# Head products in two steps of 256 tokens, eight gating products on VectorE, two gate projections in score banks

## The chip, the cores and the metric

The kernel runs on one core of one Trainium2 chip. The metric is the device time of one execution in microseconds (us). TensorE is called PE, VectorE DVE, ScalarE ACT, GpSimd POOL, SyncE SP.

## The reference

Two layers over 1024 tokens of width 1024, each wrapped as `x <- x + rmsnorm(mixer(rmsnorm(x)))`. Layer 0 is sliding-window attention (16 query heads of 64, 2 key heads, window 128, a sink per head, rotation of a quarter of each head), layer 1 a gated recurrence of 8 heads. The change lies in layer 0:

```
def attention_mixer(h, positions, w_in, b_in, sinks, w_out, b_out):
    proj = h @ w_in + b_in
    q, k, v, z = jnp.split(proj, [ATTN_WIDTH, ATTN_WIDTH + KV_WIDTH, ATTN_WIDTH + 2 * KV_WIDTH], axis=-1)
    q = partial_rope(q.reshape(B, T, N_HEADS, HEAD_DIM), positions)
    k = partial_rope(k.reshape(B, T, N_KV_HEADS, HEAD_DIM), positions)
    v = v.reshape(B, T, N_KV_HEADS, HEAD_DIM)
    o = sliding_window_gqa(q, k, v, sinks)
    return (o * jax.nn.silu(z)) @ w_out + b_out
```

## The kernel before

Every float32 operand of a matmul is split into a high and a low part in a rounded format, `hi` and `lo`, and every product is three matmuls: hi by hi, hi by lo, lo by hi (`product`, L185 to L189).

**Weights.** They are 132 slices of 128 x 512 (256 KB). `fetch` (L131 to L135) loads them over SP's queue into four raw buffers `wraw`. `advance` (L137) splits a slice: POOL makes `whi` for the first 20 slices (L152), ACT afterwards; DVE makes `wlo` (L155), POOL for slices 2 and 3. The parts go to ten places `whi`, `wlo`; `used` frees a place after its last product and advances.

**Activations.** The 1024 tokens are two halves of 512. A half is loaded as four tiles of 128 rows (`x_load`, L254; the fourth in two pieces), squared on ACT (L976), turned into `rstd` on POOL (`rstd_of`, L215 and L217) and scaled on DVE (`norm_rows`). `transpose_half` (L232 to L240) then transposes it on PE, four blocks to a PSUM bank `pst`, for eight blocks k of the model width; `act_from_psum` evicts each as `acth` (ACT, L179) and `actl` (DVE, L180).

**Products.** `proj_feat` holds weights fixed and moves 512 tokens: 24 matmuls of 128 x 512 into one of two PSUM banks tagged `mm`. The units are `v_unit` (values), `q_unit` (queries; their parts `qh`, `ql` go to DRAM, `qd`), `k_unit`, `z_unit` (gate). There are also two banks each with tags `t`, `s` and `o`; those with `s` hold the attention's scores.

**Head.** At the end of `emit` (L960 to L985) stand the loads of constants, positions and the first half of x, a flag by which the program branches, the squares and `rstd` of all four tiles, and the loads of the first four slices. Behind the branch come the norms, all 32 transposes, then `v_unit(0)` and `q_unit(0, 1, 0)`, which use slices 0, 1 and 2, 3. The loads of the other half of x, `xh`, are issued right behind the branch.

**Attention and gate.** `attn(g, b)` works on one of two groups of heads and one of eight blocks of 128 queries: scores (L528, L529), softmax, transposes, masks as four to six selects on POOL (L560 to L568), products with the values (L571 to L575), and the output `ob` (L576, L577). Other units are put between the blocks by a list (`fill`, `at`). `z_unit(p, half)` makes the gate's 128 columns p for one half: ACT's tanh (L483), `th` scaled on POOL (L484), DVE's product with z (L488), and the product with the output, `o * th`, on POOL (L490). The units p = 4 to 7 for half 0 are the last ones; where p >= 4 and half 1, the gate comes first and `attn` multiplies by the output afterwards, again on POOL (L579).

The instruction order of each engine comes from a scheduler, which places instructions by priority and readiness; `tc.high_priority` lifts some. A wrapper `v` keeps DVE's instructions in the order of the program. Each engine takes its instructions in order.

Of the kernel before, what the change touches and what calls it, by code (L numbers as in the profile page):

```python
# [12 lines left out]
F32 = mybir.dt.float32  # L13
# [5 lines left out]
ALU = mybir.AluOpType  # L19
# [70 lines left out]
def emit(tc, I, out):  # L90
    nc = tc.nc
    v = InOrder(tc, nc.vector)
    from contextlib import ExitStack
    top = ExitStack()
    with top:
# [32 lines left out]
        W_K = 10  # L128
        W = {"split": 0, "fetch": 0, "left": {}, "place": {}, "dmas": {}, "split_ins": {}, "actl": {}, "free": list(zip(whi, wlo))}

        def fetch(end):  # L131
            while W["fetch"] < min(end, NS):
                f = W["fetch"]
                W["dmas"][f] = nc.sync.dma_start(wraw[f % NR], I["w"][f])
                W["fetch"] += 1  # L135

        def advance(end=NS):  # L137

            while W["split"] < end:
                i = W["split"]  # L140
                fetch(i + NR)
                if i in (W_K, W_K + 1):
                    W["place"][i] = W["keys"][i - W_K]
                elif W["free"]:
                    W["place"][i] = W["free"].pop(0)
                else:
                    return
                raw, (hi, lo) = wraw[i % NR], W["place"][i]
                with hp():
                    on_pool = i in (2, 3)  # L150
                    if i < 20:
                        nc.gpsimd.tensor_scalar(hi, raw, 1.0, 1.0, op0=ALU.mult, op1=ALU.mult)  # L152
                    else:
                        nc.scalar.activation(hi, raw, AF.Copy)  # L154
                    W["split_ins"][i] = (nc.gpsimd if on_pool else v).tensor_tensor(lo, raw, hi.bitcast(F32), op=ALU.subtract)  # L155
                W["split"] += 1
# [19 lines left out]

        def act_from_psum(k, half, ps, scale):
            hi, lo = act[k, half]
            ins = nc.scalar.activation(hi, ps, AF.Copy, scale=scale)  # L179
            W["actl"][k] = v.scalar_tensor_tensor(lo, ps, scale, hi.bitcast(F32), op0=ALU.mult, op1=ALU.subtract)  # L180
            return ins
# [8 lines left out]

        def proj_feat(first, half):

            ps = mm()
# [17 lines left out]
        def rstd_of(pool, ms, width, eps=EPS, pinned=False):  # L211

            m = pool.tile([P, width], F32, tag="ms", bufs=4, name="ms")
            keep = tc.keep_in_program_order if pinned else lambda ins: ins
            keep(nc.gpsimd.tensor_scalar(m, ms, eps, 1.0, op0=ALU.add, op1=ALU.mult))  # L215
            r = pool.tile([P, width], F32, tag="rstd", bufs=4, name="rstd")
            W["rstd"] = keep(nc.gpsimd.tensor_tensor(r, m, nhalf[:, :width], op=ALU.pow))  # L217
            return r
# [34 lines left out]

        def x_load(xh, half):  # L254
            for j in range(4):
# [85 lines left out]
        def layer0():  # L341
# [15 lines left out]

            def q_unit(g, ct, half):
                ps = proj_feat(12 + 2 * ct if g else 2 * ct if ct else 8, half)
                with hp():  # L360
# [24 lines left out]
            with pool("start", "right") as sp:  # L385
# [5 lines left out]
                at = iter([1, 2, 3, 4])  # L391
                some = lambda: [steps.pop(0)() for _ in range(next(at))]
                with tc.high_priority(offset=1000):
                    v.on = True
                    hn0 = []
                    for j in range(4):
                        some()
                        for cs in halves(j):
                            norm_rows(sp, o0[:, j, cs], o0[:, j, cs], rs0[j])
                        hn0.append(o0[:, j, :])  # L400
# [36 lines left out]

                def v_unit(half):
                    ps = proj_feat(0, half)
                    vf = qp.tile([P, 512], F32, tag="th", bufs=2, name="vf")  # L440
# [26 lines left out]

                v_unit(0)
                q_unit(0, 1, 0)
                transpose_half(hn1, 1, C_PRE)  # L470
# [7 lines left out]
            with pool("att", "right") as ap:  # L478
                def z_unit(p, half):
                    ps = proj_feat(20 + 2 * (p ^ 4), half)  # L480
                    with hp():
                        th = qp.tile([P, 512], F32, tag="th", bufs=2, name="th")
                        nc.scalar.activation(th, ps, AF.Tanh, bias=hbias[:, 10 + p:11 + p], scale=0.5)  # L483
                        nc.gpsimd.tensor_scalar(th, th, 0.5, 0.5, op0=ALU.mult, op1=ALU.add)  # L484
                        o = og[p // 4][:, p % 4, half * 512:(half + 1) * 512]

                        early = p >= 4 and half == 1
                        v.scalar_tensor_tensor(o if early else th, ps, bias(10 + p), th, op0=ALU.add, op1=ALU.mult)  # L488
                        if not early:
                            nc.gpsimd.tensor_tensor(o, o, th, op=ALU.mult)  # L490

# [15 lines left out]
                def attn(g, b):  # L507
# [70 lines left out]
                    if g and b >= 4:  # L578
                        nc.gpsimd.tensor_tensor(ogb, ogb, ob, op=ALU.mult)  # L579

# [389 lines left out]
        v.tensor_copy(flag, ld[:1, :1])  # L970
        rs0 = []
        for j in range(4):
            ms = const.tile([P, 2], F32, tag="ss2", bufs=4, name="ss2")
            cut = halves(j)
            for i, cs in enumerate(cut):
                nc.scalar.activation(wraw[2 + j % 2].bitcast(BF16)[:, cs], o0[:, j, cs], AF.Square, scale=D ** -0.5,  # L976
                                     accum_out=ms[:, i:i + 1])
            if len(cut) > 1:
                nc.gpsimd.tensor_scalar(ms[:, :1], ms[:, :1], EPS, 1.0, op0=ALU.add, op1=ALU.mult)
            rs0.append(rstd_of(const, ms[:, len(cut) - 1:len(cut)], 1, ms[:, :1] if len(cut) > 1 else EPS))  # L980
        fetch(NR)
        go = nc.values_load(flag[0:1, 0:1])
# [79 lines left out]
```

## Time and profile before

| what | us |
| --- | --- |
| median of 3 runs | 911.94 (910.14 to 912.55) |
| profiled execution | 911.3 |
| its span in the trace | 909.5 |
| PE busy | 885.2 (97%) |
| DVE, ACT, POOL busy | 553.8, 378.1, 341.3 |

The profile is one execution. Times in it count from the span's start. A row of a timeline has the start, the duration, the engine and line, what is written from what, the shape, and in brackets the idle time before it with what ended it. A row of a group has the count, the busy time and mean nanoseconds of one, and the idle before. A row of the waits has the total, the count and the longest.

### The profile page before, as it was taken

To read this page: it belongs to the slowest core of one execution; us is meant where nothing else is said; L and a number is where in the kernel's file an instruction comes from. 1 tells how busy PE (TensorE), PEld (TensorE's weight loads), DVE (VectorE), ACT (ScalarE), POOL (GpSimd) and SP (SyncE) were. 2 spreads that over 40 slices of the span, in tenths; PEclk is the share of its full clock that TensorE was granted. 3 is DMA by queue.
4 is the path that set the end of the run, shared out by engine and by line. 5 is a ranking of instruction groups with operands and counts; after the bars stand their busy time and mean duration, and the time that the engine had idled before them with its cause. 6 is when DMAs were issued, how large, how long until landed. Compare 5 with 4: busy or idle time off the path is not lost.

```text
span 909.5 us, 14370 instructions
## 1 busy us (share of the span) xinstructions
PE 885.2 (97%) x5342; PEld 737.4 (81%) x5342; DVE 553.8 (61%) x911; ACT 378.1 (42%) x982; POOL 341.3 (38%) x506
## 2 busy tenths in 40 slices
PE   5999999999999999999999999999999999999996
PEld 4888888888887788878888888888888788888885
DVE  6879888777776435762268774246867924252343
ACT  6526667666666332542323341433334224251311
POOL 5514456658787103330054432115425433220011
PEclk9999999999999999999999999999999999999998
DMA  8546364522212223540311010121111002032053
GB/s 286 156 145 185 104 185 129 150 56 82 82 45 58 92 74 129 171 150 12 109 54 37 25 47 1 51 67 35 36 48 48 1 1 93 1 105 82 24 184 120
DMA packets 53608, 78.63 MB, mean 86 GB/s; under 512 B 4824, under 2 KB 25048, under 8 KB 53528
## 3 DMA queue, kind: packets, MB, share of 16 engines
q1 hardware_dynamic: 53248, 77.48, 27.7%
q8 instruction: 44, 0.72, 0.3%
q14 instruction: 36, 0.29, 0.1%
q10 hardware_dynamic: 280, 0.13, 0.1%
HBM read 58.89 MB, written 16.88 MB: 83 GB/s over the span
## 4 chain that ended last, share of the span: by engine, by line
PE 73%; POOL 8%; DVE 8%; issue 5%; ACT 2%; DMA 2%; SPq 0%; POOLq 0%; ACTq 0%; DVEq 0%
PE psmm L189 61%; POOL rstd L217 2%; PE psk L851 1%; PE pso L864 1%; PE pss L528 1%; PE pss L529 1%; PE pso L866 1%; POOL ms L215 1%; PE pst L549 1%; POOL mY L560 1%; POOL mY L563 1%; DVE actl L180 1%; PE pst L845 1%; PE pst L878 1%; ACT sm L543 1%
## 5 line engine op out<-in xcount | busy, mean ns | idle before, releaser
L189 PE MATMUL psmm<-acth,whi 128*128 128x512 f32 x528 | 209.0, 396 | 2.1 <-DVE th L488 1.0
L189 PE MATMUL psmm<-acth,wlo 128*128 128x512 f32 x528 | 207.9, 394 | 0.2 <-POOL wlo L155 0.2
L189 PE MATMUL psmm<-actl,whi 128*128 128x512 f32 x528 | 207.7, 393 | 0.0
L189 PE MATMUL psmm<-whi,acth 128*128 128x512 f32 (+1 forms) x520 | 202.8, 391 | 1.2 <-DVE y L630 0.6
L189 PE MATMUL psmm<-whi,actl 128*128 128x512 f32 (+1 forms) x520 | 201.2, 388 | 0.0
L189 PE MATMUL psmm<-wlo,acth 128*128 128x512 f32 (+1 forms) x520 | 200.9, 387 | 0.0
L155 DVE TENSOR_TENSOR wlo<-wraw,whi 128x512 fp32r<-128x512 f32 x126 | 95.0, 765 | 92.8 <-ACT whi L154 86.2
L189 PEld LDWEIGHTS psmm<-acth,whi 128*128 128x128 f32 x528 | 99.2, 188 | 23.2 <-DVE th L488 2.2
L189 PEld LDWEIGHTS psmm<-whi,acth 128*128 128x128 f32 x520 | 97.7, 188 | 21.7 <-DVE y L630 0.9
L189 PEld LDWEIGHTS psmm<-acth,wlo 128*128 128x128 f32 x528 | 99.2, 188 | 19.8 <-POOL wlo L155 0.6
L189 PEld LDWEIGHTS psmm<-whi,actl 128*128 128x128 f32 x520 | 97.7, 188 | 20.3 <-DVE actl L607 0.6
L189 PEld LDWEIGHTS psmm<-actl,whi 128*128 128x128 f32 x528 | 99.2, 188 | 18.0
L189 PEld LDWEIGHTS psmm<-wlo,acth 128*128 128x128 f32 x520 | 97.8, 188 | 19.0
L154 ACT ACTIVATE whi<-wraw 128x512 fp32r<-128x512 f32 x112 | 70.2, 631 | 83.9 <-PE psmm L189 65.7
L543 ACT ACTIVATE sm<-sm,st 128x129 f32<-128x129 f32 x128 | 50.0, 393 | 55.6 <-DVE st L541 55.6
L712 POOL TENSOR_SCALAR gate<-gate,lbt 128x512 f32<-128x512 f32 x16 | 17.8, 1112 | 118.9 <-ACT gate L710 108.3
L925 DVE TENSOR_TENSOR y<-psmm,wpost 128x512 f32<-128x512 f32 (+1 forms) x17 | 11.2, 660 | 53.4 <-ACT jk L924 50.0
L217 POOL TENSOR_TENSOR rstd<-ms,nhalf 128x1 f32<-128x1 f32 (+1 forms) x48 | 41.5, 864 | 3.8
L560 POOL TENSOR_SCALAR_AFFINE_SELECT mY<-pT 64x256 fp32r<-64x256 f32 x56 | 29.3, 524 | 33.6 <-ACT pT L552 28.6
L924 ACT ACTIVATE jk<-psmm 128x512 f32<-128x512 f32 (+1 forms) x17 | 9.7, 573 | 66.7 <-PE psmm L189 66.7
L179 ACT ACTIVATE acth<-pst,cst 128x512 fp32r<-128x512 f32 x48 | 29.7, 694 | 12.8 <-PE pst L237 12.8
L528 PE MATMUL pss<-KH,QS 128*128 128x256 f32 (+1 forms) x128 | 32.8, 284 | 0.4 <-DMA QS<-qd 0.4
(219 smaller groups left out, 1426.2 us busy)
## 6 DMA issues: line engine op xcount, KB each, us to landing
wraw<-in_w SPq DMA_DIRECT2D x132, 256.0 KB
QS<-qd SPq DMA_DIRECT2D x16, 512.0 KB
xr<-in_x SPq DMA_DIRECT2D x8, 512.0 KB
x1d<-xn SPq DMA_DIRECT2D x8, 512.0 KB
xr<-x1d SPq DMA_DIRECT2D x8, 512.0 KB
out_dram<-xn SPq DMA_DIRECT2D x16, 256.0 KB
xh<-in_x SPq DMA_DIRECT2D x4, 512.0 KB
qd<-qh SPq DMA_DIRECT2D x8, 256.0 KB
```

The costliest lines, as they stand in the source:

```text
L154: nc.scalar.activation(hi, raw, AF.Copy)
L155: W["split_ins"][i] = (nc.gpsimd if on_pool else v).tensor_tensor(lo, raw, hi.bitcast(F32), op=ALU.subtract)
L179: ins = nc.scalar.activation(hi, ps, AF.Copy, scale=scale)
L180: W["actl"][k] = v.scalar_tensor_tensor(lo, ps, scale, hi.bitcast(F32), op0=ALU.mult, op1=ALU.subtract)
L189: W["mm"] = nc.tensor.matmul(ps, a, b, start=(k == 0 and i == 0), stop=(k == NK - 1 and i == 2))
L217: W["rstd"] = keep(nc.gpsimd.tensor_tensor(r, m, nhalf[:, :width], op=ALU.pow))
L528: nc.tensor.matmul(ps[:, i, :nkk], q, KH[:, g, k0:k0 + nkk], start=True, stop=False)
L543: nc.scalar.activation(sm[:, h, :], sm[:, h, :], AF.Exp, bias=nm[:, h:h + 1], scale=0.125, accum_out=dn[:, h:h + 1])
L560: nc.gpsimd.affine_select(mY[r, :, :64], src[64:, :, :64].bitcast(F32), [[0, 4], [-1, 64]], ALU.is_gt, 0.0, base=0, channel_multiplier=1)
L712: nc.gpsimd.tensor_scalar(dst, dst, ol, lb, op0=ALU.mult, op1=ALU.add)
L924: nc.scalar.activation(jk[:, c0:c1], ps, AF.Square, scale=D ** -0.5, accum_out=ss)
L925: v.tensor_tensor(y[:, c0:c1], ps, wpost[:, c * 512 + c0:c * 512 + c1], op=ALU.mult)
```

## The change

- The head's first two products are computed in two steps, `pair(0)` and `pair(1)`, of 256 tokens each, into two banks `first` with the tag `s`: 96 matmuls of 128 x 256 in place of 48 of 128 x 512. Transposes and evictions go in pairs of blocks, 128 x 256, with banks `t` and `o`.
- The first four slices are taken in the order 0, 2, 1, 3 (`FIRST`), so that both products have a slice each first. The loads are issued as x0, x1, slice 0, slice 2, x2, half of x3, slice 1, the other half of x3, slice 3. Only tiles 0 and 1 are squared ahead of the branch; the squares of tiles 2 and 3 are put between the evictions of the first step on ACT.
- ACT and POOL are kept in program order in this part too (`a`, `g`), and eight slices are split in it (`advance(8)`). The loads of `xh` are issued after those of slices 4 and 6.
- In `z_unit` with p >= 4 and half 0 (`end`) the product `o * th` is done on DVE, and for odd p the projection goes to a bank `s`. In `attn` with g = 1 and b >= 4 the product `ogb * ob` is done on DVE. These are 4 and 4 products of 128 x 512.

```diff
+    a = InOrder(tc, nc.scalar)
+    g = InOrder(tc, nc.gpsimd)
...
+        FIRST = (0, 2, 1, 3)
...
-                fetch(i + NR)
+                fetch((NR, NR + 1, NR + 1, NR + 3)[i] if i < 4 else i + NR)
+                i = FIRST[i] if i < 4 else i
...
+            def q_unit(g, ct, half, ps=None):
+                if ps is None:
+                    ps = proj_feat(12 + 2 * ct if g else 2 * ct if ct else 8, half)
...
+                first = [mm(tag="s") for _ in range(2)]
...
+                    def pair(h):
+
+                        cs = slice(256 * h, 256 * h + 256)
+                        for k in range(NK):
+                            pt = pp.tile([P, 256], F32, tag="to"[k % 2], name="pst")
+                            for j in range(2):
+                                nc.tensor.transpose(pt[:, j * P:(j + 1) * P], o0[:, 2 * h + j, k * P:(k + 1) * P], ident)
+                            last = act_from_psum(k, 0, pt, cst[:, C_PRE + k:C_PRE + k + 1], cs)
+                            if h == 0:
+                                {0: lambda: (advance(2), square0(2)), 2: lambda: advance(3), 3: lambda: (norm0(2), square0(3)), 4: lambda: advance(4)}.get(k, list)()
+                        for k in range(NK):
+                            for u in range(2):
+                                c, (hi, lo) = (k % 4) * P, act[k, 0]
+                                product(first[u][:, cs], k, weight(2 * u, k // 4, c, c + P), (hi[:, cs], lo[:, cs]))
+                                if h:
+                                    used(2 * u + k // 4)
+                        return last
...
                     advance(1)
-                    last = transpose_half(hn0, 0, C_PRE, {2: lambda: advance(4)})
+                    pair(0)
+                    norm0(3)
+                    some()
+                    some()
+                    last = pair(1)
+                    a.on = False
+                    advance(8)
+                    g.on = False
...
-                x_load(xh1, 1)
+                for f in (4, 6):
+                    with tc.issue_after(W["dmas"][f].ins):
+                        x_load(xh1, 1, range(f - 4, f - 2))
...
-                v_unit(0)
-                q_unit(0, 1, 0)
+                v_unit(0, first[0])
+                q_unit(0, 1, 0, first[1])
...
-                    ps = proj_feat(20 + 2 * (p ^ 4), half)
+
+                    end = p >= 4 and half == 0
+                    ps = proj_feat(20 + 2 * (p ^ 4), half, "s" if end and p % 2 else "mm")
...
-                            nc.gpsimd.tensor_tensor(o, o, th, op=ALU.mult)
+                            (v if end else nc.gpsimd).tensor_tensor(o, o, th, op=ALU.mult)
...
-                        nc.gpsimd.tensor_tensor(ogb, ogb, ob, op=ALU.mult)
+                        v.tensor_tensor(ogb, ogb, ob, op=ALU.mult)
...
-        x_load(o0, 0)
+        x_load(o0, 0, range(2))
+        for f in FIRST[:2]:
+            nc.sync.dma_start(wraw[f], I["w"][f])
+        x_load(o0, 0, range(2, 3))
...
+        rs0 = [row_rstd0(const, j, wraw[FIRST[2 + j]].bitcast(BF16)) for j in range(2)]
+        for f in FIRST[2:]:
+            nc.sync.dma_start(wraw[f], I["w"][f])
+        x_load(o0, 0, range(3, 4))
```

In the rows below a number behind a name is that of the buffer: `acth_0_104` and `actl_0_105` are the first block k of the first half, `acth_0_108` the second. In the kernel before `whi_80` to `whi_83` are slices 0 to 3. In the changed one they are slices 0, 2, 1 and 3, with `wlo_90` to `wlo_93` beside them, and `whi_84` to `whi_87` are slices 4 to 7. `wraw_100` to `wraw_103` are the four raw buffers, `o_136` is the first half of x.

PE of the kernel before, right behind the branch:

```order
L237 MATMUL pst<-cst,o_136 128x128 x24
L189 MATMUL psmm<-acth_0_104,whi_80 128x512
L189 MATMUL psmm<-acth_0_104,whi_82 128x512
L237 MATMUL pst<-cst,o_136 128x128 x4
L189 MATMUL psmm<-actl_0_105,whi_80 128x512
L189 MATMUL psmm<-acth_0_104,wlo_90 128x512
```

PE of the changed kernel, where the first step ends and the second begins:

```order
L195 MATMUL psmm<-acth_0_132,wlo_93 128x256
L419 MATMUL pst<-cst,o_136 128x128 x5
L195 MATMUL psmm<-acth_0_104,whi_80 128x256
L195 MATMUL psmm<-acth_0_104,whi_81 128x256
L195 MATMUL psmm<-acth_0_104,whi_84 128x512
L419 MATMUL pst<-cst,o_136 128x128 x2
L195 MATMUL psmm<-actl_0_105,whi_80 128x256
L195 MATMUL psmm<-acth_0_104,wlo_90 128x256
L195 MATMUL psmm<-actl_0_105,whi_81 128x256
L195 MATMUL psmm<-acth_0_104,wlo_91 128x256
L195 MATMUL psmm<-acth_0_108,whi_80 128x256
L195 MATMUL psmm<-acth_0_108,whi_81 128x256
```

Before, the third unit's matmuls (`whi_84`) come only after all 48 of the first two; now one of them stands inside the second step, and three rows further follow `actl_0_105,whi_84` and `acth_0_104,whi_86`, a product of slice 6 for a still later unit.

SP of the kernel before, from the first slices' loads on:

```order
L134 DMA wraw_102<-in_w 128x512
L134 DMA wraw_103<-in_w 128x512
L982 TENSOR_LOAD flag
L987 COMPARE_AND_BRANCH
L258 DMA xh_329<-in_x 128x1024 x4
L326 DMA m_391<-in_msk 128x256
L134 DMA wraw_102<-in_w 128x512
L134 DMA wraw_103<-in_w 128x512
L134 DMA wraw_100<-in_w 128x512
L134 DMA wraw_101<-in_w 128x512
```

SP of the changed kernel at the same place:

```order
L1034 TENSOR_LOAD flag
L1039 COMPARE_AND_BRANCH
L332 DMA m_515<-in_msk 128x256
L136 DMA wraw_100<-in_w 128x512
L136 DMA wraw_102<-in_w 128x512
L264 DMA xh_465<-in_x 128x1024 x4
L136 DMA wraw_101<-in_w 128x512
L136 DMA wraw_103<-in_w 128x512
L136 DMA wraw_100<-in_w 128x512
```

The four loads of `xh` now stand behind slices 4 and 6 and ahead of slices 5 and 7.

POOL of the changed kernel, behind the branch:

```order
L87 TENSOR_TENSOR wlo_91<-wraw_102,whi_81 128x512
L87 TENSOR_SCALAR ms<-ss_229 128x1
L87 TENSOR_TENSOR rstd<-ms,nhalf 128x1
L87 TENSOR_SCALAR whi_82<-wraw_101 128x512
L87 TENSOR_SCALAR ss_254<-ss_254 128x1
L87 TENSOR_SCALAR ms<-ss_254 128x1
L87 TENSOR_TENSOR rstd<-ms,nhalf 128x1
L87 TENSOR_SCALAR whi_83<-wraw_103 128x512
L87 TENSOR_TENSOR wlo_93<-wraw_103,whi_83 128x512
L87 TENSOR_SCALAR whi_84<-wraw_100 128x512
L87 TENSOR_SCALAR whi_85<-wraw_101 128x512
L87 TENSOR_SCALAR whi_86<-wraw_102 128x512
```

The `rstd` of tiles 2 and 3 stood ahead of all four `whi` before, and stand between the slices now.

POOL of the kernel before, in the last part of the attention (`og_971` holds the outputs of the second group of heads):

```order
L568 AFFINE_SELECT pT<-pT 128x8x64
L484 TENSOR_SCALAR th<-th 128x512
L490 TENSOR_TENSOR og_971<-og_971,th 128x512
L560 AFFINE_SELECT mY<-pT 64x4x64
L563 AFFINE_SELECT mY<-pT 64x4x64
L560 AFFINE_SELECT mY<-pT 64x4x64
L563 AFFINE_SELECT mY<-pT 64x4x64
L566 AFFINE_SELECT pT<-pT 128x8x64
L568 AFFINE_SELECT pT<-pT 128x8x64
L579 TENSOR_TENSOR og_971<-og_971,ob 128x4x128
L484 TENSOR_SCALAR th<-th 128x512
```

DVE of the changed kernel at that place (`og_1045` is the same tile):

```order
L533 SCALAR_TENSOR_TENSOR th<-psmm,cst,th 128x512
L622 TENSOR_TENSOR ob<-pso,ob 64x512
L533 SCALAR_TENSOR_TENSOR th<-psmm,cst,th 128x512
L535 TENSOR_TENSOR og_1045<-og_1045,th 128x512
L598 TENSOR_TENSOR pT<-pst,pT 128x512
L652 TENSOR_TENSOR actl_0_105<-o_136,acth_0_104 128x512
L624 TENSOR_TENSOR og_1045<-og_1045,ob 128x4x128
L652 TENSOR_TENSOR actl_0_109<-o_136,acth_0_108 128x512
L535 TENSOR_TENSOR og_1045<-og_1045,th 128x512
L598 TENSOR_TENSOR pT<-pst,pT 128x512
```

The products of L490 and L579 have left POOL's order, and stand on DVE as L535 and L624, ahead of `pT` and between the `actl` pieces of the output projection.

More of the change, by code (lines that the diff above doesn't have):

```diff
@@ L128, in emit @@
         W_K = 10
-        W = {"split": 0, "fetch": 0, "left": {}, "place": {}, "dmas": {}, "split_ins": {}, "actl": {}, "free": list(zip(whi, wlo))}
+        W = {"split": 0, "fetch": 0, "left": {}, "place": {}, "dmas": {}, "split_ins": {}, "free": list(zip(whi, wlo))}
         def fetch(end):
@@ L175, in emit, with act_from_psum @@
         o0 = const.tile([P, 4, T], F32, name="o0")
[L177 to L180, printed above, removed]
+        def act_from_psum(k, half, ps, scale, c=slice(0, 512)):
+            hi, lo = (x[:, c] for x in act[k, half])
+            ins = a.activation(hi, ps, AF.Copy, scale=scale)
+            v.scalar_tensor_tensor(lo, ps, scale, hi.bitcast(F32), op0=ALU.mult, op1=ALU.subtract)
             return ins
@@ L252, in halves, with x_load @@
             return [slice(0, 512), slice(512, D)] if t == 3 else [slice(0, D)]
-        def x_load(xh, half):
-            for j in range(4):
+        def x_load(xh, half, rows=range(4)):
+            for j in rows:
                 t = half * 4 + j
```

45 lines of the change are left out of this document (22 added, 23 removed).

## The prediction

> **What bounds the kernel now.** I read the page first, then the waits of PE, then PE's timeline in the three places where it loses time.
>
> ```profile
> span 909.5 us, 14370 instructions
> ...
> PE 885.2 (97%) x5342; PEld 737.4 (81%) x5342; DVE 553.8 (61%) x911; ACT 378.1 (42%) x982; POOL 341.3 (38%) x506
> ...
> GB/s 286 156 145 185 104 185 129 150 56 82 82 45 58 92 74 129 171 150 12 109 54 37 25 47 1 51 67 35 36 48 48 1 1 93 1 105 82 24 184 120
> ```
>
> PE is busy for 97% of the span, so the time is PE's work plus the moments in which PE waits. The work is not cut by this change: only waits can go or come. The waits of PE, with the longest at the right:
>
> ```profile
> PE psl L967 <- DVE ld L965: 5.5, 1, 5.5
> PE pst L237 <- DVE o L87: 3.0, 1, 3.0
> PE pso L571 <- POOL pT L568: 1.6, 4, 0.6
> PE psmm L189 <- DVE th L488: 1.5, 3, 0.7
> ```
>
> The first two are the loading of x and the first norm, which both kernels have. The next two lie in the last part of the attention, where POOL is late with the masked scores (L568) and the gate's two product banks are held until `th` has been read (L488). The head is in PE's timeline:
>
> ```profile
> 8.92 5.38 PE L237 MATMUL pst<-cst,o 128*128 128x128 f32 x24 [3.00 <-DVE o L87]
> 14.42 0.47 PE L189 MATMUL psmm<-acth,whi 128*128 128x512 f32 x1
> 15.35 0.50 PE L189 MATMUL psmm<-acth,whi 128*128 128x512 f32 x1 [0.45 <-POOL whi L152]
> ...
> 17.38 0.50 PE L189 MATMUL psmm<-acth,wlo 128*128 128x512 f32 x1 [0.17 <-POOL wlo L155]
> ...
> 18.62 0.39 PE L189 MATMUL psmm<-acth,wlo 128*128 128x512 f32 x1
> ...
> 31.56 0.39 PE L189 MATMUL psmm<-acth,whi 128*128 128x512 f32 x1
> 31.79 1.47 PE L237 MATMUL pst<-cst,xh 128*128 128x128 f32 x12
> ```
>
> From 18.62 to 31.56 lie 57 steps, so a 512-wide matmul costs PE 0.227 us from start to start; a transpose at most 1.47 / 12 = 0.12, and I take 0.11. The shape that the change brings, 256 wide, stands in the attention:
>
> ```profile
> 266.70 0.28 PE L528 MATMUL pss<-KH,QS 128*128 128x256 f32 x1
> ...
> 267.41 0.28 PE L528 MATMUL pss<-KH,QS 128*128 128x256 f32 x1
> ...
> 267.06 0.19 PEld L528 LDWEIGHTS pss<-KH,QS 128*128 128x128 f32 x1
> ```
>
> Six steps in 0.71 us: 0.118 each, half of 0.227 and 0.004 more.
>
> **The head.** Two steps of 256 tokens let the products start before rows 2 and 3 of x are normed. The supply of the weights decides what that is worth, and it is POOL's:
>
> ```profile
> 7.86 1.04 POOL L217 TENSOR_TENSOR rstd<-ms,nhalf 128x1 f32<-128x1 f32 x1
> 12.71 3.17 POOL L152 TENSOR_SCALAR whi<-wraw 128x512 fp32r<-128x512 f32 x4 [0.19 <-issue]
> 16.03 2.99 POOL L155 TENSOR_TENSOR wlo<-wraw,whi 128x512 fp32r<-128x512 f32 x2
> 24.74 2.81 POOL L152 TENSOR_SCALAR whi<-wraw 128x512 fp32r<-128x512 f32 x4
> L179 ACT ACTIVATE acth<-pst,cst 128x512 fp32r<-128x512 f32 x48 | 29.7, 694 | 12.8 <-PE pst L237 12.8
> L180 DVE SCALAR_TENSOR_TENSOR actl<-pst,cst,acth 128x512 fp32r<-128x512 f32 x40 | 27.9, 742 | 6.4 <-ACT acth L179 6.4
> ```
>
> Now POOL goes on after the second rstd at 8.9. It does two `whi` at 0.79 (3.17 / 4), hbias (at most 0.2 in the row's gap before 16.03) and one `wlo` at 1.5 (2.99 / 2), with 0.2 for the branch: 12.4, where before the first `whi` began at 12.7. But the rstd of rows 2 and 3, `whi_82`, `whi_83` and `wlo_93` follow on the same in-order POOL: 2 x 0.79 + 1.5, and five small instructions that I put at 2.0 (the rstd above takes 1.04, the others less): `wlo_93` at 17.5. The last 12 half products of the first step wait for it. After them PE has 7 transposes, 8 half products and two full ones up to the row that I name next: 24 halves' worth x 0.118 + 7 x 0.11 = 3.6. The first eviction of the second step has nothing to cover it, some 0.9: half of 0.69 on ACT, half of 0.74 on DVE and their hand-overs. PE is through at 17.5 + 3.6 + 0.9 = 22.0.
>
> There it meets a product of a later unit that stands inside the second step: `psmm<-acth_0_104,whi_86`. On POOL `whi_86` comes after `whi_85`, and `whi_85` needs slice 5. On SP slice 5 now stands behind the four loads of the second half of x: they take 2.1 MB, with the slice 2.36 MB. Two rates and a landing:
>
> ```profile
> 16.00:20.00 4.00, 3.83 (x20) 2.88 (x19) 4.00 (x7) 3.17 (x6) 3.02 (x3) 1.00 0.96 385
> 14.00:22.00 8.00, 7.26 (x34) 5.44 (x34) 7.93 (x13) 7.11 (x13) 6.11 (x10) 1.00 0.96 350
> 32.69 2.97 DMA wraw<-in_w
> ```
>
> The columns are stretch, sum, PE, PEld, DVE, ACT, POOL busy, clock, DMA share, GB/s. Slice 6 is asked for when `wlo_91` frees its buffer at 12.4 and lands 2.97 later, at 15.4. Then 2.36 MB at 385 to 350 GB/s take 6.1 to 6.7: slice 5 lands at 21.5 to 22.1. `whi_85` and `whi_86` at 0.70 (2.81 / 4) make it 22.9 to 23.5, and I take 23.2.
>
> What had before done by then? At the row of 17.38 it had begun 6 of the 30 matmuls' worth (56 / 2 + 2) and done 28 transposes, where the new order has 26: the same point came at 17.38 + 24 x 0.227 - 2 x 0.11 = 22.6. So the head loses 0.6, and the 40 half products that remain cost 40 x 0.0035 = 0.14 more: **+0.75**. Behind PE's wait for `whi_86` stands everything of the second step, since PE takes its rows in order. Were slice 5 early, PE would come at 22.0 and the head would gain 0.46; were my supply of the first half a microsecond too slow as well, 1.4. In the other direction each microsecond of the slice is a microsecond.
>
> **Two waits behind it.**
>
> ```profile
> 42.31 0.40 PE L189 MATMUL psmm<-acth,wlo 128*128 128x512 f32 x1
> 42.99 0.47 PE L189 MATMUL psmm<-acth,whi 128*128 128x512 f32 x1 [0.28 <-DVE ql L378]
> ...
> 64.20 0.39 PE L189 MATMUL psmm<-acth,whi 128*128 128x512 f32 x1
> 65.01 0.41 PE L528 MATMUL pss<-KH,QS 128*128 128x128 f32 x2 [0.42 <-DMA QS<-qd]
> ```
>
> They cost 0.68 - 0.23 = 0.45 and 0.81 - 0.23 = 0.58. The first is a wait for one of the two product banks; the first two products now lie in score banks, so the turn of the banks is two units further and the wait should go. The second hangs on the writes of q to DRAM, whose place among SP's rows shifts, with a load of the values now between: I take a quarter of it as gained. Together **-0.6**, bounds 0 and -1.0.
>
> **The gate.** Stretch 240 to 300:
>
> ```profile
> 240.00:300.00 60.00, 57.30 (x274) 45.35 (x272) 45.83 (x76) 36.54 (x95) 48.21 (x64) 1.00 0.19 55
> L579 POOL TENSOR_TENSOR og<-og,ob 128x512 f32<-128x512 f32 x4 | 5.2, 1292 | 1.9 <-DVE ob L577 1.9
> L490 POOL TENSOR_TENSOR og<-og,th 128x512 f32<-128x512 f32 x3 | 5.1, 1695 | 2.6 <-DVE th L488 1.7 <-DVE st L541 0.9
> L560 POOL TENSOR_SCALAR_AFFINE_SELECT mY<-pT 64x256 fp32r<-64x256 f32 x14 | 8.1, 581 | 2.9 <-ACT pT L552 1.7 <-DVE pT L553 0.4
> L373 DVE TENSOR_TENSOR qf<-qf,qtB 128x512 f32<-128x512 f32 x4 | 3.0, 744 | 0.1
> ```
>
> POOL is busy 48.2 of 60 here and bursts of it make PE wait; DVE is busy 45.8. The change takes 4 x 1.29 and 4 x 1.70 from POOL, 12.0 us, and gives DVE eight products at 0.74 (the nearest row: two f32 inputs in SBUF, same shape), 5.9 us: DVE comes to 51.7 of 60, still with room. On DVE's in-order queue the products stand ahead of `pT` and `actl` pieces, which then come 0.74 later at most four times; POOL's selects, which wait for `pT`, start that much later but no longer find a product of 1.3 to 1.7 ahead of them.
>
> What PE loses there is more than the idle that is listed:
>
> ```profile
> 244.09 0.50 PE L571 MATMUL pso<-pT,VX 128*128 128x512 f32 x1 [0.38 <-POOL pT L568]
> ...
> 272.65 0.40 PE L189 MATMUL psmm<-acth,wlo 128*128 128x512 f32 x1
> 273.25 0.50 PE L571 MATMUL pso<-pT,VX 128*128 128x512 f32 x1 [0.20 <-POOL pT L568]
> ...
> 281.39 0.48 PE L189 MATMUL psmm<-actl,whi 128*128 128x512 f32 x1
> 282.49 0.50 PE L571 MATMUL pso<-pT,VX 128*128 128x512 f32 x1 [0.62 <-POOL pT L568]
> ```
>
> From start to start 273.25 is late by 0.60 - 0.23 = 0.37 (0.20 listed), 282.49 by 1.10 - 0.23 = 0.87 (0.62 listed): about 0.2 above each listed wait. Seven waits with 1.6 + 1.5 listed make 3.1 + 7 x 0.19 = 4.4. The one at 244.09 (0.38 + 0.16 = 0.54) comes behind products of the first four gate parts, which POOL keeps: it stays. Of the remaining 3.9 I count 3.6, since the three bank waits go with the score banks outright and the three waits for selects go with POOL's products: **-3.6**, bounds -0.8 (only the bank that is used twice helps) and -4.4.
>
> The Trainium skill, on its page "SBUF — State Buffer", section "Who interferes with whom", says that a VectorE instruction with two SBUF inputs and a GpSimd instruction that reads SBUF shut each other out for the whole instruction. By it the moved products would each hold POOL for up to their own length, which is the second rival. The trace agrees in part: POOL's two kinds of product of one shape differ, 1.29 and 1.70.
>
> **Sum.** 0.75 - 0.6 - 3.6 = -3.45. The profiled execution took 911.3 (909.5 of span and 1.8 around it), 0.6 below the median; against its own time that is 907.85, and the median 911.94 becomes 908.5.
>
> **Rivals.** (1) *The head eats the rest.* Slice 5 comes later than the two rates say: at 270 GB/s 2.36 MB take 8.7, `whi_86` is ready at 25.5, 2.3 later: 910.8. For it: the queue's four loads may not be dense. Against: the 385 GB/s of the row for 16 to 20, which is this very traffic before.
>
> (2) *The products hold POOL.* Eight spans of 0.74 in which POOL's selects stand: of 12.0 relief 6.1 is left, half, and the gate gives 1.8: 910.3. For it: selects in this stretch take 581 ns, and 1.29 against 1.70 for one product. Against: DVE already runs 45.8 of 60 here, so that what it costs POOL is largely in the rows.
>
> (3) *Slower: PE stands at `whi_86`.* If the queue runs at the rate of the page's second slice, 156 GB/s, slice 5 lands at 15.4 + 15.1 = 30.5, `whi_86` is ready at 31.9, 8.7 later than I take: 917.2. It decides when `whi_86` is ready after 23.2 + 3.45 + 2.74 = 29.4, thus when the queue is under 2.36 / 12.6 = 187 GB/s. Against: that slice had less to move, and the rows in which the queue was full read 350 and 385.
>
> (4) *Slower: weight loads come to light.* Each half product has a load of its own: 48 more of 0.19. If they were not covered, 9.0 us: 917.5. Against: in the row above the load takes 0.19 while the matmuls of 256 start every 0.118. The Trainium skill's page "TensorE: Matmul & The Clock Gate", section "The mechanism", states that a weight load overlaps matmuls in flight only when it goes to another row group, which would bring this case about; the trace contradicts it.
>
> **How the numbers follow.** Forecast 0.58, its own range 905.4 to 909.2; rivals 0.18, 0.16, 0.06 and 0.02. The low end is the best of the three terms, 911.94 - 1.4 - 1.0 - 4.4 = 905.1. The high end takes in the first two rivals and the case that nothing is gained: 912.4. What is left out is the two slow rivals, 0.08, and a tail of the forecast. About 0.3% (2.74 us) is what a measurement of this kernel can tell from no change: faster is below 909.2, which is the forecast's case, 0.58; rivals 1 and 2 lie within it, 0.34; 3 and 4 beyond, 0.08.
>
> **What would show it.** In the profile after: PE's first product near 11, before 14.4; a listed wait of PE for POOL's `whi` of 0.3 to 1.5 around 22 to 24; the row for `th` among PE's waits gone and that for L568's selects down to one or two; POOL in the stretch before 300 down by 10 and DVE up by 6; the first product behind the attention about 3.5 earlier. A wait for `whi` of over 3 would make the head's step wrong, waits for selects that stay at 1.6 the gate's, a step over 0.13 between the half products both.

## The result and the profile after

The changed kernel takes 917.04 us (916.32 to 919.97, 6 runs) against 912.02 (910.14 to 912.55, 6 runs) for the kernel before: ratio 1.0064, 95% interval 1.005 to 1.0078. It is 5.0 us slower, where the forecast was 908.5, and it lies above the high end of the range, 912.4. The page and PE's waits of the changed kernel (L87 is the helper that keeps an engine in program order):

```profile
span 915.4 us, 14477 instructions
...
PE 888.0 (97%) x5390; PEld 742.5 (81%) x5390; DVE 559.9 (61%) x927; ACT 378.7 (41%) x990; POOL 330.7 (36%) x498
```

```profile
PE pso L616 <- POOL pT L613: 2.9, 6, 1.0
...
PE pss L573 <- DVE sm L581: 2.0, 2, 1.7
PE pst L594 <- ACT pT L597: 1.4, 1, 1.4
...
PE psmm L195 <- POOL whi L87: 0.5, 1, 0.5
```

POOL has lost 10.6 us of work as foreseen, and the row for `th` is gone, but the wait for POOL's selects has grown from 1.6 to 2.9, and two waits are new: scores that wait for their bank to be read (L573) and transposes that wait for theirs (L594). The head, in PE's timeline of the changed kernel:

```profile
11.21 0.77 PE L195 MATMUL psmm<-acth,whi 128*128 128x256 f32 x2
...
22.07 0.39 PE L195 MATMUL psmm<-actl,whi 128*128 128x512 f32 x1
22.95 0.50 PE L195 MATMUL psmm<-acth,whi 128*128 128x512 f32 x1 [0.49 <-POOL whi L87]
...
27.04 0.28 PE L195 MATMUL psmm<-actl,whi 128*128 128x256 f32 x1
...
28.48 0.28 PE L195 MATMUL psmm<-actl,whi 128*128 128x256 f32 x1
...
64.87 0.41 PE L573 MATMUL pss<-KH,QS 128*128 128x128 f32 x2 [0.16 <-DMA QS<-qd]
...
65.90 0.28 PE L574 MATMUL pss<-KL,QS 128*128 128x128 f32 x1
```

and the eighth score of the kernel before, to set beside that last row:

```profile
66.28 0.27 PE L529 MATMUL pss<-KL,QS 128*128 128x128 f32 x1
```

The wait for `whi_86` stands at 22.95 with 0.49, and 12 steps of half products take 1.44 (27.04 to 28.48), 0.120 each. The first scores come at 64.87; before they came at 65.01, with one product fewer done. At the eighth score both have done the same 192 products (two halves counted as one): it starts at 65.90 now and at 66.28 before. Up to there the change is worth 0.38. That is not clear of the spread between executions, for the kernels with the old head that are timed below start their eighth score anywhere from 65.46 (`b_gate`) to 67.08 (`b_dve`). The 5 us are lost behind it. Five stretches of the changed kernel, and two of them in the kernel before (columns: stretch, sum, PE, PEld, DVE, ACT, POOL busy, clock, DMA share, GB/s):

```profile
120.00:140.00 20.00, 19.11 (x99) 15.61 (x98) 13.40 (x26) 10.97 (x32) 7.45 (x16) 1.00 0.50 149
260.00:280.00 20.00, 15.29 (x80) 12.07 (x79) 17.18 (x31) 11.47 (x33) 13.59 (x22) 1.00 0.28 77
275.50:279.50 4.00, 0.89 (x6) 0.61 (x6) 3.50 (x9) 3.68 (x10) 2.20 (x5) 1.00 0.59 157
280.40:286.80 6.40, 5.99 (x16) 4.34 (x16) 4.83 (x12) 4.21 (x19) 3.93 (x7) 0.50 0.16 41
280.00:300.00 20.00, 19.59 (x81) 15.78 (x80) 15.05 (x27) 14.15 (x36) 11.09 (x18) 0.83 0.14 40
```

```profile
120.00:140.00 20.00, 19.96 (x110) 16.82 (x109) 16.50 (x34) 14.04 (x44) 10.16 (x21) 1.00 0.55 155
260.00:280.00 20.00, 19.51 (x97) 15.67 (x97) 16.88 (x28) 13.00 (x36) 16.22 (x22) 1.00 0.27 74
```

PE is idle for 0.9 of 20 us in the first stretch and for 4.7 in the second, and just behind that it works at half its clock. How PE stands still there, with the rows of DVE and ACT that it waits for, all of the changed kernel:

```profile
275.18 0.39 PE L195 MATMUL psmm<-acth,wlo 128*128 128x512 f32 x1
277.01 0.63 PE L594 MATMUL pst<-cst,sm 128*128 128x128 f32 x4 [1.44 <-ACT pT L597]
279.31 0.39 PE L573 MATMUL pss<-KH,QS 128*128 128x256 f32 x1 [1.68 <-DVE sm L581]
...
280.99 0.79 PE L616 MATMUL pso<-pT,VX 128*128 128x512 f32 x1 [0.27 <-POOL pT L613]
...
283.36 0.63 PE L195 MATMUL psmm<-actl,whi 128*128 128x512 f32 x1
283.79 0.63 PE L195 MATMUL psmm<-acth,wlo 128*128 128x512 f32 x1
...
287.11 0.39 PE L195 MATMUL psmm<-actl,whi 128*128 128x512 f32 x1
287.34 0.39 PE L195 MATMUL psmm<-acth,wlo 128*128 128x512 f32 x1
```

```profile
276.35 0.57 ACT L597 ACTIVATE pT<-pst 128x512 fp32r<-128x512 f32 x1
278.81 0.78 DVE L581 COPY_PREDICATED sm<-msk,pss 128x256 f32<-128x256 uint8 x2
```

In PE's order there stand ten products, four transposes, eight scores, four products with the values, and then 26 products in a row (282.77 to 290.76). Between the transposes and the values nothing stands that PE could do while the softmax goes through ACT, DVE and POOL: the 26 products come behind. PE stands for 1.44 and 1.68, and then its steps are 0.43 apart (283.36, 283.79) where 0.23 is usual, until 287.

In 120 to 140 it is DVE whose order is unlucky. Its timeline in the changed kernel:

```profile
124.25 0.67 DVE L161 TENSOR_TENSOR wlo<-wraw,whi 128x512 fp32r<-128x512 f32 x1
129.35 0.75 DVE L385 SCALAR_TENSOR_TENSOR ql<-psmm,cst,qh 128x512 fp32r<-128x512 f32 x1 [4.43 <-DMA qd<-ql]
130.02 0.17 DVE L590 RECIPROCAL st<-st 128x4 f32<-128x4 f32 x1
```

A `ql` waits 4.43 for an earlier one to be written to DRAM, and the reciprocal of the softmax stands behind it; PE meets that as waits for `sm` and for POOL's selects from 132 on:

```profile
132.76 0.39 PE L573 MATMUL pss<-KH,QS 128*128 128x256 f32 x1 [0.37 <-DVE sm L581]
...
134.71 0.50 PE L616 MATMUL pso<-pT,VX 128*128 128x512 f32 x1 [0.51 <-POOL pT L613]
```

To compare kernels I use one measure, PE's loss: for each of PE's instructions the time from its start to the next one's, less the median of that for its shape, summed over a stretch of the profiled execution. It holds idle, half clock and hand-overs alike.

| kernel | 0 to 40 | 40 to 120 | 120 to 160 | 240 to 320 |
| --- | --- | --- | --- | --- |
| before | 4.2 | 1.8 | 0.7 | 6.4 |
| changed | 4.5 | 0.7 | 2.4 | 11.2 |

The differences, 0.4 - 1.1 + 1.7 + 4.8, make 5.7; the two spans differ by 5.9. The match is better than the table deserves: in 160 to 240 and behind 320 the changed kernel loses 0.5 less each, and against that stand terms outside the measure, about 0.5 of them for the half products (96 x 0.119 against 48 x 0.227). The two stretches behind 120 hold the loss in any case.

### The profile page after: what moved, and what is told of

It is laid out like the page before. It is cut to its first block, busy times and chain, and to the rows that moved or that the text cites. A ratio compares the mean times of both kernels' runs of the same rounds, so it can differ in the third digit from the quotient of the medians.

```text
span 915.4 us, 14477 instructions
## 1 busy us (share of the span) xinstructions
PE 888.0 (97%) x5390; PEld 742.5 (81%) x5390; DVE 559.9 (61%) x927; ACT 378.7 (41%) x990; POOL 330.7 (36%) x498
## 4 chain that ended last, share of the span: by engine, by line
PE 74%; DVE 10%; POOL 5%; issue 4%; DMA 4%; ACT 2%; SPq 0%; ACTq 0%; POOLq 0%; DVEq 0%
PE psmm L195 62%; POOL rstd L223 2%; PE psk L896 1%; PE pso L909 1%; PE pso L911 1%; PE pss L573 1%; PE pss L574 1%; ACT sm L588 1%; POOL ms L221 1%; DMA qd<-ql 1%; PE pst L594 1%; DMA QS<-qd 1%; PE pst L890 1%; PE pst L923 1%; DMA wraw<-in_w 1%
## 5 line engine op out<-in xcount | busy, mean ns | idle before, releaser
L195 PE MATMUL psmm<-acth,whi 128*128 128x512 f32 (+1 forms) x544 | 210.9, 392 | 1.1 <-POOL whi L87 0.5
L195 PE MATMUL psmm<-actl,whi 128*128 128x512 f32 (+1 forms) x544 | 211.1, 389 | 0.0
L195 PE MATMUL psmm<-acth,wlo 128*128 128x512 f32 (+1 forms) x544 | 210.9, 389 | 0.2 <-DVE wlo L161 0.2
L161 DVE TENSOR_TENSOR wlo<-wraw,whi 128x512 fp32r<-128x512 f32 x122 | 91.4, 761 | 91.8 <-ACT whi L160 88.1
L195 PEld LDWEIGHTS psmm<-acth,whi 128*128 128x128 f32 x544 | 102.3, 190 | 22.1 <-DVE qf L749 0.9
L195 PEld LDWEIGHTS psmm<-acth,wlo 128*128 128x128 f32 x544 | 103.0, 189 | 19.4 <-DVE wlo L161 0.4
L195 PEld LDWEIGHTS psmm<-actl,whi 128*128 128x128 f32 x544 | 103.2, 190 | 18.2
L970 DVE TENSOR_TENSOR y<-psmm,wpost 128x512 f32<-128x512 f32 (+1 forms) x17 | 11.2, 660 | 53.2 <-ACT jk L969 50.2
L605 POOL TENSOR_SCALAR_AFFINE_SELECT mY<-pT 64x256 fp32r<-64x256 f32 x56 | 28.5, 509 | 40.6 <-ACT pT L597 31.3
L608 POOL TENSOR_SCALAR_AFFINE_SELECT mY<-pT 64x256 fp32r<-64x256 f32 x64 | 31.5, 492 | 12.2 <-ACT pT L597 5.7
L573 PE MATMUL pss<-KH,QS 128*128 128x256 f32 (+1 forms) x128 | 32.7, 286 | 2.2 <-DVE sm L581 2.0
```

The costliest lines, as they stand in the source:

```text
L161: W["split_ins"][i] = (g if on_pool else v).tensor_tensor(lo, raw, hi.bitcast(F32), op=ALU.subtract)
L195: W["mm"] = nc.tensor.matmul(ps, a, b, start=(k == 0 and i == 0), stop=(k == NK - 1 and i == 2))
L573: nc.tensor.matmul(ps[:, i, :nkk], q, KH[:, g, k0:k0 + nkk], start=True, stop=False)
L605: nc.gpsimd.affine_select(mY[r, :, :64], src[64:, :, :64].bitcast(F32), [[0, 4], [-1, 64]], ALU.is_gt, 0.0, base=0, channel_multiplier=1)
L608: nc.gpsimd.affine_select(mY[r, :, 64:], src[:64, :, 64:].bitcast(F32), [[0, 4], [1, 64]], ALU.is_ge, 0.0, base=0, channel_multiplier=-1)
L970: v.tensor_tensor(y[:, c0:c1], ps, wpost[:, c * 512 + c0:c * 512 + c1], op=ALU.mult)
```

## The experiments

The theories named in the expectations: A, the score banks of the gate; B, the products on DVE; C, the head alone shifts the attention; later D, the order that the scheduler gives the attention, against E, the head's transfers and banks as such. Each ratio is against runs of the kernel before on the same chip. PE's losses are always those of the one execution that was profiled.

**The new head alone** (`a_head`), gate edits undone:

```diff
-                    ps = proj_feat(20 + 2 * (p ^ 4), half, "s" if end and p % 2 else "mm")
+                    ps = proj_feat(20 + 2 * (p ^ 4), half)
...
-                            (v if end else nc.gpsimd).tensor_tensor(o, o, th, op=ALU.mult)
+                            nc.gpsimd.tensor_tensor(o, o, th, op=ALU.mult)
...
-                        v.tensor_tensor(ogb, ogb, ob, op=ALU.mult)
+                        nc.gpsimd.tensor_tensor(ogb, ogb, ob, op=ALU.mult)
```

> The changed kernel with its gate edits undone: all eight products on POOL, all gate projections in the two product banks; the head as changed. Theory A (the two projections in score banks, under the new head, are planned behind the scores, so that blocks of the attention run with no products between them): the 5 us that PE loses more in 240 to 300 go, the 1.7 more in 120 to 160 stay: 912 to 914. Theory B (the eight products on VectorE hold up its queue): the same 912 to 914. Theory C (the new head alone shifts the attention against the products, and the gate edits have no part): 916 to 918.

Measured 916.61, ratio 1.0055 (1.0041 to 1.0068). Theory C: the head alone makes as large a slowdown as the whole change, 5.0. Its waits:

```profile
PE pso L616 <- POOL pT L613: 3.7, 5, 2.0
...
PE psmm L195 <- DVE ql L385: 1.3, 1, 1.3
```

The wait for `ql` is a single one, at 131.7. PE's loss is 4.7, 0.3, 4.2 and 9.6 in the four stretches: 0.5 more in the head and 1.5 less just behind it, then 3.5 and 3.2 more far behind. The granted clock reads 1.00 over its stretch 240 to 320, so this kernel is as slow as the changed one without any half clock there.

**The changed kernel without score banks for the gate** (`a_dve`): the first of the three edits above alone.

> The changed kernel with the two gate projections back in the product banks; the eight products stay on VectorE. Theory A: the loss of 240 to 300 falls from 11 to 4 to 6 us: 910 to 912.5. Theory B: it stays, 916 to 918. Theory C: 916 to 918.

Measured 913.27, ratio 1.002 (1.001 to 1.003), which lies outside the ranges of all three theories. Its profiled execution was the fastest, 911.27.

**The changed kernel with the products back on POOL** (`a_bank`): the second and third edit alone.

> The changed kernel with the eight products back on POOL; the two projections stay in score banks. Theory A: as slow as the changed kernel or slower, 916 to 920, with stretches of several us before 285 in which PE waits for the softmax chain. Theory B: 912 to 914. Theory C: 916 to 918.

Measured 919.02, ratio 1.0083 (1.007 to 1.0097). Two waits of PE in it:

```profile
272.17 0.58 PE L616 MATMUL pso<-pT,VX 128*128 128x512 f32 x1 [2.03 <-POOL pT L613]
...
283.71 1.09 PE L594 MATMUL pst<-cst,sm 128*128 128x128 f32 x4 [3.69 <-ACT sm L577]
```

Under the new head the score banks thus cost: against the kernel before on the same chip, 1.7 slower becomes 5.0 with the products on DVE, and 5.0 becomes 7.4 with them on POOL. The products on DVE gain. PE's loss in 240 to 320 is 5.6 without the banks and 13.0 with the banks alone, against 11.2 for the changed kernel. Theory A holds for a part, B is out, and neither explains `a_head`.

**The old head with the gate edits** (`b_gate`):

```diff
...
-                    ps = proj_feat(20 + 2 * (p ^ 4), half)
+                    end = p >= 4 and half == 0
+                    ps = proj_feat(20 + 2 * (p ^ 4), half, "s" if end and p % 2 else "mm")
...
-                            nc.gpsimd.tensor_tensor(o, o, th, op=ALU.mult)
+                            (v if end else nc.gpsimd).tensor_tensor(o, o, th, op=ALU.mult)
...
-                        nc.gpsimd.tensor_tensor(ogb, ogb, ob, op=ALU.mult)
+                        v.tensor_tensor(ogb, ogb, ob, op=ALU.mult)
```

> The kernel before with the gate edits alone: eight products on VectorE, two projections in score banks; the old head. The prediction's gate term says 3.6 less, 908.4. Theory A, in which the score banks hurt only under the new head's plan: 908 to 911. Theory B: over 914. Theory C: 908 to 911.

Measured 907.74 against 911.60, ratio 0.996 (0.9946 to 0.9973): 3.9 faster. In its stretch 240 to 300 and its wait for the selects, beside 48.2 us of POOL's work and 1.6 of wait in the kernel before:

```profile
240.00:300.00 60.00, 58.59 (x286) 48.14 (x285) 53.53 (x88) 38.60 (x97) 39.57 (x55) 1.00 0.28 82
```

```profile
PE pso L572 <- POOL pT L569: 1.0, 3, 0.5
```

The gate term of the prediction was right, under the old order of the attention.

**That order.** Compared instruction by instruction, PE's order from the first scores to the end of the attention is the same in the kernel before and in `b_gate` but for a few products in the last blocks; in the changed kernel and in `a_head` it is another from the first block on: behind the first eight scores come 25 products where the old order has 22, and so it goes on. The next six kernels are edits that give one order or the other. One of them concerns the pinned split: `advance(8)` in the head, by which slices 4 to 7 are split in the program's order on POOL.

**The changed kernel without the pinned split** (`n_gate`), old order:

```diff
                     a.on = False
-                    advance(8)
                     g.on = False
```

> The changed kernel without the pinned split of slices 4 to 7 (advance(8)); nothing else is touched, but the scheduler then gives the attention the same order on PE as under the old head. Theory D (the head's own work costs little; what costs 5 us is that the scheduler lays the attention's steps and the products between them in another order, which loses about 3.5 in 120 to 160 and 3 in 240 to 310): 907 to 909.5, the loss in 120 to 160 under 1, in 240 to 300 3 to 4. Theory E (the new head's transfers and banks themselves make later steps late, whatever the order): 912 to 917.

Measured 914.48, ratio 1.004 (1.0026 to 1.0054), outside what theory D had said and inside E's 912 to 917. By place it is D's only in part: the loss in 240 to 320 is 3.0, as D said, but in 120 to 160 it is 1.7, where D said under 1, and 0 to 40 loses 12.1, which neither had named. PE's waits:

```profile
PE pst L243 <- DVE xh L87: 2.9, 1, 2.9
...
PE pst L496 <- POOL vmid L489: 1.8, 1, 1.8
```

Without the pinned split POOL does `rstd` of the second half first, and slices 4 to 7 only from 33.4 on:

```profile
32.44 1.29 POOL L223 TENSOR_TENSOR rstd<-ms,nhalf 128x1 f32<-128x1 f32 x1
33.42 3.37 POOL L158 TENSOR_SCALAR whi<-wraw 128x512 fp32r<-128x512 f32 x4
```

PE has run out of products by then, and its clock reads 0.50 from 31.3 to 37.9, which is part of the 12.1.

**The new head alone without the pinned split** (`h_noadv`) is the same edit on `a_head`:

> The new head alone (gate edits undone) and without the pinned split. Attention in the order of the kernel before. Theory D: what the head is worth by itself, 911 to 913 against 911.6 to 912 for the kernel before; my term for it was +0.75, and -0.6 for the two waits behind it. Theory E: 914 to 917.

Measured 917.37, ratio 1.0069 (1.0056 to 1.0083): again 11.7 lost in 0 to 40, but 0.7 in 120 to 160 and 6.6 in 240 to 320, where the kernel before has 0.7 and 6.4. The expected time missed, since I had not seen that the split itself was needed; by place, D is borne out, and E is not: both score banks are used in this head too, and behind 40 nothing is lost to them.

**The changed kernel with its first two products in product banks** (`m_gate`), pinned split kept, old order:

```diff
-                first = [mm(tag="s") for _ in range(2)]
+                first = [mm() for _ in range(2)]
```

> The changed kernel with the first two products in the product banks in place of the score banks; the pinned split stays. The attention's order on PE is again that under the old head. Theory D: 907 to 910, as without the pinned split, though another edit was taken away. Theory E, if the split and its transfers are the cause: 914 to 917.

Measured 908.62, ratio 0.9973 (0.9963 to 0.9983), as D said. The profiled execution was its slowest, 910.3; there the head pays 7.3 in 0 to 40, with a wait that the profile puts down to `ms`, the first step of POOL's `rstd` of the second half:

```profile
PE psmm L195 <- POOL ms L221: 1.3, 1, 1.3
```

**The loads of the second half of x not held back** (`h_xh`), on the new head alone, new order:

```diff
-                for f in (4, 6):
-                    with tc.issue_after(W["dmas"][f].ins):
-                        x_load(xh1, 1, range(f - 4, f - 2))
+                x_load(xh1, 1)
```

> The new head alone (gate edits undone) with the loads of the second half of x issued without waiting for slices 4 and 6; pinned split kept, and the attention in the new order. Theory D: as slow as the new head alone, 915.5 to 918, and the losses in 120 to 160 and 240 to 310 unchanged. Theory E, if those transfers are the cause: 911 to 914.

Measured 915.21, ratio 1.0049 (1.0036 to 1.0063), a little under what D said. The loss in 240 to 320 stays, 9.7; in 120 to 160 it is 2.1, not 4.2, so there the timing of the transfers has a part. For the selects it waits as long as the new head alone:

```profile
PE pso L614 <- POOL pT L611: 3.7, 5, 2.0
```

**One tag altered** (`v_sm`), the changed kernel in everything else, old order:

```diff
-                first = [mm(tag="s") for _ in range(2)]
+                first = [mm(tag="s"), mm()]
```

> The changed kernel with one tag altered: the second of the first two products lies in a product bank, the first stays in a score bank. Head, pinned split and gate edits are kept; PE's order up to the first scores is nearly that of the changed kernel, but behind them the scheduler lays the attention as in the kernel before. Theory D (the order costs it): 905.5 to 908.5, 8 to 11 less than the changed kernel, with under 1 lost in 120 to 160 and 3 to 4 in 240 to 300. Theory E (the head's transfers or banks make later steps late): 913 to 917.

Measured 907.29 against 911.19, ratio 0.996 (0.9948 to 0.9972), as D said and not E. This is the test that decides: PE's rows up to the first scores are nearly those of the changed kernel, the gate edits are all there, and it is 9.8 faster by the medians, 8.9 if each is first set against the kernel before on its own chip (+5.0 and -3.9). Its page, stretches and waits:

```profile
span 905.4 us, 14479 instructions
...
PE 883.6 (98%) x5390; PEld 740.5 (82%) x5390; DVE 558.1 (62%) x927; ACT 379.7 (42%) x990; POOL 329.8 (36%) x498
```

```profile
120.00:140.00 20.00, 20.00 (x111) 17.14 (x110) 16.47 (x34) 13.29 (x43) 10.15 (x22) 1.00 0.54 158
240.00:300.00 60.00, 58.64 (x287) 48.12 (x286) 53.54 (x88) 38.98 (x98) 39.89 (x56) 1.00 0.26 79
```

```profile
PE pss L573 <- DMA QS<-qd: 1.0, 1, 1.0
PE pso L616 <- POOL pT L613: 0.9, 2, 0.5
```

Its losses are 4.4, 1.5, 0.4 and 3.1. It does better than both kernels, but not measurably better than `b_gate` with the old head: both have a ratio of 0.996, so the new head has no gain that these runs can tell.

**Three pinned slices** (`v_adv7`), old order:

```diff
-                    advance(8)
+                    advance(7)
```

> The changed kernel with three slices split ahead in pinned order in place of four (advance(7)): slice 7 is split later. The attention is laid as in the kernel before. Without any of the four the head waited 8.3 in 20 to 40. Theory D: attention as in the kernel without the pinned split, and the head loses between 0.5 and 4, by when slice 7 is split: 906 to 911.

Measured 911.72, ratio 1.0003 (0.9993 to 1.0014), just outside D's 906 to 911. The attention is as in `v_sm`, 0.4 and 2.9, and the head loses 5.0. But 40 to 120 loses 5.3: the first scores now wait for q from DRAM, which D had not foreseen, and the clock reads 0.57 over 69 to 73, just behind. The wait:

```profile
PE pss L573 <- DMA QS<-qd: 2.6, 1, 2.6
```

**The two gate edits apart, under the old head.** `b_dve` has the products on DVE alone, `b_bank` the score banks alone (the edits of `b_gate`, one kind each).

> The kernel before with the eight products on VectorE alone; no score banks for the gate. PE's order is the same as with both gate edits up to 300. Both gate edits together gave -3.9 against the kernel before. If the products carry it: -2.5 to -4, 907.5 to 909.5. If the three waits for banks (2.0 of the 4.4 lost) carry half: -1.5 to -2.5.

> The kernel before with two gate projections in score banks alone; the products stay on POOL. If the banks carry half of the gain: -1.5 to -2.5. If the products carry it: 0 to -0.8, since the waits for POOL's selects stay and the bank waits only move.

`b_dve` measured 907.88, ratio 0.9964 (0.9952 to 0.9977), `b_bank` 908.76, ratio 0.9973 (0.9963 to 0.9983). Waits of the one and then of the other:

```profile
PE pss L529 <- DMA QS<-qd: 1.6, 1, 1.6
...
PE pso L572 <- POOL pT L569: 0.5, 1, 0.5
```

```profile
PE pso L572 <- POOL pT L569: 2.3, 4, 1.6
```

The products bring -3.3, the banks -2.4, both -3.9: they take away the same waits by two ways, so that the second adds little. With the banks alone the waits for `th` go, but POOL's products remain, and one wait for the selects grows to 1.6. The first expectation is met; the second lies at the edge of the half that it named.

**All fourteen kernels side by side.** PE's loss in 240 to 320, by the state of the gate and the order of the attention:

| gate | new order | old order |
| --- | --- | --- |
| as before | 9.6, 9.7 | 6.4, 6.6 |
| products on DVE | 5.6 | 3.0 |
| score banks | 13.0 | 4.0 |
| both | 11.2 | 2.7 to 3.1 (five kernels) |

In every row the new order loses more, whichever edit gives the old one. The score banks save 2.4 under the old order (6.4 to 4.0) and cost 3.4 under the new one (9.6 to 13.0). In 120 to 160 the new order loses 1.8 to 4.2 and the old one 0.4 to 0.8, except for `n_gate` with 1.7, so there the two are less cleanly apart.

## Why the prediction was wrong

- **The head**, +0.75: measured 0.4 more lost in 0 to 40, with the wait at 22.95 where `whi_86` was put at 23.2. Right in mechanism and place, somewhat too large, and in PE's own arrival by two errors that nearly cancel: `wlo_93` was done at 18.0, not 17.5, and the first eviction of the second step cost 0.4, not 0.9. The extra of a half product was also reckoned too small. By the prediction's own steps it is 0.0045, not 0.0035; by the measured 0.120 it is 0.0065, so 0.26 for the 40 and not 0.14.
- **The two waits behind it**, -0.6: 1.1 less lost in 40 to 120. Right in sign: the wait for `ql` is gone and that for q fell from 0.42 to 0.16. The size is not sure, since kernels with the old head lose 1.5 to 2.8 there. The whole change up to the eighth score brings a gain of 0.38, where the two terms made 0.15 of loss: off by 0.5.
- **The gate**, -3.6: the old head with the gate edits shows -3.9, and 3.3 less PE loss in 240 to 320. Right as long as the attention keeps its order, though the waits for the selects fell only to 1.0 there. In the changed kernel the same stretch lost 4.8 more, and the prediction's own sign against the gate came: the waits for the selects did not fall from 1.6 but grew to 2.9.
- **The step that failed** is the sum itself: "0.75 - 0.6 - 3.6" has terms for the places where the kernel before loses time and none for the 240 us between, on the ground that "only waits can go or come", as though waits came only where an edit is. The edit of the head made the scheduler lay out the whole attention otherwise, and that cost 1.7 in 120 to 160 and, with the gate edits, 4.8 in 240 to 320; with one tag altered, `v_sm`, the old order and 907.3 come back. The change of order could be read off beforehand, PE's order against PE's order; I read it in the head and in the gate's rows of POOL and DVE, not in PE's rows of the attention. There, "the three waits for selects go with POOL's products" took for granted that PE still has products between transposes and values.
- **The rivals.** The third gave 917.2, close to the measured time, by luck, for its mechanism did not happen: PE stood at `whi_86` for 0.49, not for 8.7. The first, the same wait made 2.3 longer, did not come either. The second (products that hold POOL) would have made the gate's gain 1.8; `b_gate` shows 3.9, and `b_dve`, the products alone, 3.3. The fourth (weight loads of the half products) would show as steps over 0.13; they are 0.120.
- **No term for the clock.** The half clock behind the long stop costs about as much as the stop: from 280.4 to 286.8 PE works at 0.50, so about 3.2 of 6.4 us, and the two gaps before cost 1.6 and 1.8 (starts 275.18 to 277.01 and 277.4 to 279.31, less a step). It is not what makes the change slow as such, since `a_head` loses its 5.0 with the clock at 1.00 there.

What stays open: why the scheduler changes its plan with the tag of one bank, or with the eighth pinned slice. The runs show that its plan decides, not by what rule it flips; and only PE's order was compared. That order and loss go together rests on five kernels with the new order and nine with the old, made by different edits; an exchange of the order with every edit of the changed kernel kept was not tried. `h_xh` shows besides that in 120 to 160 the timing of the transfers has a part of its own.

## What to carry to other kernels

Where a scheduler lays out the instructions, an edit in one place can reorder work hundreds of microseconds away: compare the whole order of the engine that bounds the time, before and after, ahead of any sum over edits, and price the stretches where fill work between dependent steps gets thinner. If two edits are bundled, time each alone and look at the order of each; here one tag decided between 917 and 907. And measure two cures for one wait together as well as apart: they do not add.

## What the runs showed of the hardware

PE's granted clock fell to half after a stop that was not one piece: by the stretches above PE was busy for 0.9 of 4 us in 275.5 to 279.5, and from 280.4 to 286.8 the clock read 0.50 and 512-wide matmuls started 0.43 apart. A single stop of 2.02 in `a_head`, before 273.81, left the clock at 1.00. The Trainium skill, page "TensorE: Matmul & The Clock Gate", section "What's actually happening", states that an idle window of about 3.4 us halves the clock until a busy window has passed; the trace agrees with the halving. It shows it with a short run of transposes between the two stops, and the half clock lasted at least 6.4 us.
